# Making the second pass's V weight factors in the first pass's V stage instead of its heads

## The chip, the cores and the metric

The kernel runs on one core of a Trainium2 chip. The metric is the device time of one execution in microseconds; the median of a few runs is compared.

## The reference

One layer of a hybrid decoder block over 2048 tokens of width 1024, batch 1, all in float32. Cut to what matters here:

```python
h = rms_norm(x, g_pre) * (1.0 + scale) + shift
(pv, pg, hq, hf, hi, hg, mg_pool, mg_hgrn) = split(h @ w_in, ...)
pooled = einsum(multiscale_pool(pv), pool_w) * pool_scale
branch_a = (pooled * silu(pg)) @ w_pool_o
f = lb + (1 - lb) * sigmoid(hf);  k = 1 - f;  q = silu(hq);  v = hi
o = hgrn2(q, k, v, log(f))                    # gated linear recurrence, 8 heads of 128
branch_b = (rms_norm(o, hgrn_norm_g) * silu(hg)) @ w_hgrn_o
merged = sigmoid(mg_pool) * branch_a + sigmoid(mg_hgrn) * branch_b
x = x + gate * rms_norm(merged @ w_out, g_post)
```

The slice `hi` of `h @ w_in` (columns 3072 to 4095 of `w_in`, `O_I` in the kernel) is the V of the recurrence.

## The kernel before

The 2048 tokens are worked in two passes (`p` = 0, 1) of 1024, each pass in two halves (`t` = 0, 1) of 512. A pass goes through stages: V (the product that gives `hi`), the eight heads (for each the products for its gates, and the recurrence), A and B (the two output projections), and Y (`w_out` and the sum).

**Split products.** To keep float32 accuracy, each operand is split into a high and a low part: `split` (L175) casts to float32r on ScalarE (ACT) and subtracts on VectorE (DVE). A product of 128x128 by 128x512 then takes three matmuls on TensorE (PE), all issued at L331. Weights are loaded raw (tiles `wr`, pool of 7 buffers, L179), split into tiles `whl` (pool of 4 buffers) four items ahead of their use (`LOOK = 4`), and where the second pass needs them again, stored to DRAM.

**Fewer products.** In the heads of both passes and in V of pass 1, seven products of half-size blocks stand for eight. The blocks of `h` for this are mixed by `h_mix` (four calls, each three or four subtractions and four splits on DVE and ACT; its tiles are `t`, `hT`, `lT`). The weights of V in pass 1 need seven factors made of four blocks of `w_in`. `row_factors` makes them: for each of 4 block rows and 2 column halves ("pairs" below, eight in all) it gives seven steps:

```python
steps += [ld, nop, lambda two=two: two((0, "11"), (1, "12")),     # L295 to L299
          lambda two=two, a=sums: two(a, (2, "s1")),
          lambda two=two, a=sums2: two(a, (3, "11")),
          lambda two=two, a=sums3: two((4, "21"), a),
          lambda two=two: two((5, "12"), (6, "22"))]
```

`ld` loads two 256 KB tiles (`rav`, `rbv`, L276); the next step is empty; each `put` casts on ACT and subtracts on DVE into a tile `rfv` and stores it to DRAM (`scr_v<-rfv`, L109); `sums`, `sums2` and `sums3` are 128x256 additions and subtractions on DVE (L461).

**Where the steps are placed.** Before the change the 56 steps are the list `behind_heads`, made just before the heads of pass 0. In the heads `htick` is called about 21 times a head and takes one step at two of every five calls:

```python
def htick():                          # L1341 to L1345
    tick()
    every[0] += 1
    if every[0] % 5 in (1, 3):
        once(behind_heads)
```

What is left after the last head is taken at once (L1387). The heads of pass 1 do the same with the factors of `w_out` (`row_factors("y7", ...)`).

**The V stage of pass 0.** It is made of jobs of two 128-row weight items each (`v_job`, 24 matmuls), four jobs (`q` = 0 to 3) to a group, a group for each `t` and each half `grp` of the columns. A group accumulates in four PSUM banks (`psV`, the pool has four); its last job copies them on ACT (`V<-psV`, L888) and stores them (`Vd<-V`). The first group runs among the kernel's preparations; the other three are the loop over `vj`, twelve jobs (n = 0 to 11). Behind the jobs of the first of them three calls of `late` follow (`h_in` for the second half: scale by `rr`, shift, and split into `hB`, `lB`), behind jobs 0, 1 and 3 of the second and 0 of the third one mix each.

**What sets the order.** The code only traces the work; the framework orders each engine's instructions and inserts the waits. Nearly all working tiles (`utile`) come from one pool of 76 buffers (`NU = 76`); a tile takes a buffer at its first write. The order on SP, which issues all transfers, is also the framework's, but for those that `gated` puts behind the last store.

Of the kernel before, what the change touches and what calls it, by code (L numbers as in the profile page):

```python
# [20 lines left out]
D = 1024  # L21
# [10 lines left out]
O_PV, O_PG, O_Q, O_F, O_I, O_G, O_MP, O_MH = 0, 512, 1024, 2048, 3072, 4096, 5120, 6144  # L32
# [4 lines left out]
FAST_V, FAST_Y = True, True  # L37
# [34 lines left out]
def tile_block(ctx: ExitStack, tc: tile.TileContext, x, c, w_ada, b_ada, g_pre, g_post, w_in,  # L72
# [3 lines left out]
    V, A, G, PE, SP = nc.vector, nc.scalar, nc.gpsimd, nc.tensor, nc.sync  # L76
    x, out = x[0], out[0]
    w_ada, w_in = w_ada[0], w_in[0]
# [14 lines left out]
    def utile(name, dt=F32):  # L93
        return up.tile([P, T], dt, tag="u", name=name)

    def dram(name, shape):
        return dp.tile(shape, F32, name=name, tag=name)
# [10 lines left out]
    def store(key, dst, src):  # L108
        last["st"] = SP.dma_start(dst, src)  # L109
# [64 lines left out]
    def split(src32, hi, lo, e=None):  # L174
        return A.copy(hi, src32), (e or V).tensor_tensor(lo, src32, hi.bitcast(F32), op=SUB)  # L175
# [80 lines left out]
    def row_factors(key, src, e):  # L256

        steps = []
        W = T // 2
        for i in range(4):  # L260
            for c0 in (0, W):
                r = {}

                def put(f, nm, i=i, c0=c0, r=r):
                    w = utile(f"rf{key}{f}{i}{c0}", F32R)
                    hi, lo = w[:, 0:W], w[:, W:T]
                    split(r[nm], hi, lo, e)
                    if (key, f, i) not in scr:
                        scr[key, f, i] = dram(f"scr_{key}_{f}_{i}", [P, 2 * T])
                    store((key, f, i), scr[key, f, i].rearrange("p (z n) -> p z n", z=2)[:, :, c0:c0 + W],  # L270
                          w.bitcast(F32).rearrange("p (z n) -> p z n", z=2))

                def ld(i=i, c0=c0, r=r):
                    a, b = utile(f"ra{key}{i}{c0}"), utile(f"rb{key}{i}{c0}")
                    for w, k in ((a, 2 * i), (b, 2 * i + 1)):
                        SP.dma_start(w.rearrange("p (z n) -> p z n", z=2),  # L276
                                     src[k * P:(k + 1) * P, :].rearrange("p (z n) -> p z n", z=2)[:, :, c0:c0 + W])
                    r.update({"11": a[:, 0:W], "21": a[:, W:T], "12": b[:, 0:W], "22": b[:, W:T]})

                def sums(r=r, i=i, c0=c0):  # L280
                    r["s1"] = utile(f"rs{key}{i}{c0}")[:, 0:W]
                    tt(r["s1"], r["21"], r["22"], op=ADD, e=e)
                    tt(r["21"], r["11"], r["21"], op=SUB, e=e)

                def sums2(r=r):
                    tt(r["11"], r["s1"], r["11"], op=SUB, e=e)

                def sums3(r=r):
                    tt(r["12"], r["12"], r["11"], op=SUB, e=e)

                def two(*fs, put=put):
                    for f in fs:
                        f() if callable(f) else put(*f)
                nop = lambda: None
                steps += [ld, nop, lambda two=two: two((0, "11"), (1, "12")),  # L295
# [4 lines that stand above are left out]
        return steps  # L300
# [159 lines left out]
    def tt(o, a, b, op=MUL, e=None):  # L460
        return (e or V).tensor_tensor(o, a, b, op=op)  # L461
# [399 lines left out]
    def v_job(p, t, grp, q, cx, hook=None):  # L861
        if q == 0:
            cx["psV"] = [bank(f"psV{p}_{t}_{grp}_{tk}") for tk in range(NT)]
        pss = cx["psV"]
        it = None

        def mul(k, w, tk):
            hh, hl = cx["mv"][("B11", "B21", "B12", "B22")[2 * t + k % 2], k // 2]
            xh, xl = hh[:, tk * P:(tk + 1) * P], hl[:, tk * P:(tk + 1) * P]
            mm(pss[tk], xh, w[0], k == 0, False)  # L870
            mm(pss[tk], xh, w[1], False, False)
            return mm(pss[tk], xl, w[0], False, k == KT - 1)

        if q < 3:
            for k2 in range(2):
                w = take(2 if p == 0 and t == 0 and grp == 0 else LOOK)
                with after(it):
                    for tk in range(NT):
                        im = mul(2 * q + k2, w, tk)
                if hook is not None:  # L880
                    it = hook(2 * q + k2, im)
            return
        ws = [take(), take(LOOK - 1)]
        for tk in range(NT):
            for k2 in range(2):
                mul(2 * q + k2, ws[k2], tk)
            vt = utile(f"V{p}_{t}_{grp}_{tk}")
            A.copy(vt, pss[tk])  # L888
            store("Vd", cx["Vd"][:, t * NT + tk, grp * T:(grp + 1) * T], vt)
# [340 lines left out]
    def once(steps):  # L1230

        if steps:
            steps.pop(0)()
# [43 lines left out]
    for p in range(NPASS):  # L1277
# [39 lines left out]
        vj = [] if p > 0 and FAST_V else [(t, grp, q) for t in range(2) for grp in range(2) for q in range(4)]  # L1317
        if p == 0:
            vj = vj[4:]
        for n, (t, grp, q) in enumerate(vj):  # L1320
            if (t, grp, q) == (1, 0, 0):
                while late:
                    once(late)
            v_job(p, t, grp, q, cx)
            if t == 0:
                for _ in range(3 if p == 0 else 1):
                    once(late)
            elif q != 2:
                once(mixes)
        while mixes:  # L1330
            once(mixes)

        psa[:] = [ph.tile([P, T], F32, tag=f"ph{i}", name=f"psa{p}_{i}") for i in range(2)]
        behind_heads = []
        if p == 0 and FAST_V:
            behind_heads += row_factors("v7", w_in[:, O_I:O_I + D], V)
        if p == NPASS - 1 and FAST_Y:
            behind_heads += row_factors("y7", w_out, V)
        every = [0]
# [111 lines left out]
```

## Time and profile before

| | us |
|---|---|
| median of 3 runs | 1799.63 (1799.39 to 1804.18) |
| the profiled execution, its own time | 1797.54 |
| its span, first to last instruction | 1795.8 |
| first V products to the heads of pass 0 | 23.9 to 123 |
| heads of pass 0 | 123 to 693.8 |
| V of pass 1 | 934 to 1016.5 |
| heads of pass 1 | 1016.5 to 1569.5 |

In the profile's rows an L number is a line of the kernel, `out<-in` are the program's tile names without their numbers, and what stands in brackets is the idle time of the engine just before, with what ended it. PE is the matmul engine, PEld its weight load, SPq the queue of transfers. The granted clock of PE was 0.999.

### The profile page before, as it was taken

What the parts mean: (1) busy time and instruction counts of PE and PEld (TensorE: products, weight loads), DVE (VectorE), ACT (ScalarE), POOL (GpSimd) and SP (SyncE); (2) the same over time, 40 slices, a digit from 0 to 9 for tenths busy, and PEclk for the clock granted to TensorE, in tenths of its full rate; (3) what the DMA queues carried; (4) which work ended last, traced back from release to release, by engine and by line L of the source; (5) the groups of instructions that cost most, each with busy time, mean ns of one, the idle gap of its engine ahead of it and who ended that gap; (6) DMA issues with size and microseconds to landing.
All of it is one profiled execution on the core that took longest, in us unless ns stands there. A gap on an engine that the chain in (4) does not pass through costs nothing.

```text
span 1795.8 us, 32263 instructions
## 1 busy us (share of the span) xinstructions
PE 1753.0 (98%) x11997; PEld 1434.1 (80%) x11997; DVE 1161.1 (65%) x2522; ACT 801.1 (45%) x1925; POOL 80.6 (4%) x144
## 2 busy tenths in 40 slices
PE   7999999999999999999999999999999999999998
PEld 4787887888787787888878788888888888888886
DVE  3758898897888895475536166666666665633446
ACT  5746657566565563222433144354454453310041
POOL 1100000000000010000000000000000000000002
PEclk9999999999999999999999999999999999999999
DMA  9768787888878769997987886876877866696367
GB/s 316 255 198 292 272 295 288 277 304 281 285 271 300 265 213 318 336 323 257 320 294 249 281 254 199 282 249 215 274 228 238 280 206 238 201 351 209 129 204 258
DMA packets 270902, 471.49 MB, mean 263 GB/s; under 512 B 21101, under 2 KB 144666, under 8 KB 270746
## 3 DMA queue, kind: packets, MB, share of 16 engines
q1 hardware_dynamic: 270746, 469.44, 77.1%
q8 instruction: 94, 1.54, 0.4%
q14 instruction: 62, 0.51, 0.1%
HBM read 275.90 MB, written 193.46 MB: 261 GB/s over the span
## 4 chain that ended last, share of the span: by engine, by line
PE 62%; DMA 5%; DVE 2%; ACT 1%; issue 1%; SPq 0%; POOL 0%; DVEq 0%; ACTq 0%
PE psB L331 10%; PE pagp L331 6%; PE pam L331 6%; PE pafq L331 5%; PE psA L331 4%; PE psy L331 4%; PE pegp L331 3%; PE pefq L331 3%; PE pem L331 3%; PE psa L331 2%; PE ray L331 2%; PE po L331 2%; PE raV L331 2%; PE pbm L331 2%; PE pbfq L331 1%; PE pbgp L331 1%
## 5 line engine op out<-in xcount | busy, mean ns | idle before, releaser
L175 ACT CAST whl<-wr 128x512 fp32r<-128x512 f32 x192 | 118.5, 621 | 131.0 <-PE psB L331 24.7
L175 DVE TENSOR_TENSOR whl<-wr,whl 128x512 fp32r<-128x512 f32 x192 | 130.9, 688 | 64.2 <-ACT whl L175 55.2
L331 PE MATMUL psB<-Gh,whl 128*128 128x512 f32 x512 | 158.6, 390 | 0.0
L331 PE MATMUL pagp<-hT,whl 128*128 128x512 f32 x384 | 128.5, 395 | 4.7 <-DVE c22gp L461 3.8
L331 PE MATMUL pam<-hT,whl 128*128 128x512 f32 x384 | 129.5, 398 | 1.2 <-DVE c22m L461 1.2
L331 PE MATMUL pafq<-hT,whl 128*128 128x512 f32 x384 | 126.7, 391 | 3.3 <-ACT c12fq L592 3.3
L331 PEld LDWEIGHTS psB<-Gh,whl 128*128 128x128 f32 x512 | 96.1, 188 | 20.5 <-issue 0.5
L690 DVE COPY_PREDICATED PT<-mask,psa 128x256 f32<-128x256 uint8 x160 | 86.4, 550 | 36.1 <-PE psa L331 36.0
L331 PE MATMUL psB<-Gl,whl 128*128 128x512 f32 x256 | 100.0, 391 | 0.0
L331 PEld LDWEIGHTS pagp<-hT,whl 128*128 128x128 f32 x384 | 72.0, 188 | 21.9 <-issue 3.1
L331 PEld LDWEIGHTS pafq<-hT,whl 128*128 128x128 f32 x384 | 72.1, 188 | 19.5 <-ACT c12fq L592 4.4
L331 PEld LDWEIGHTS pam<-hT,whl 128*128 128x128 f32 x384 | 72.1, 188 | 17.2 <-DVE c22m L461 1.6
L331 PE MATMUL psA<-Ph,whl 128*128 128x512 f32 x256 | 82.5, 397 | 3.1 <-DMA Ph<-Pd 1.9
L331 PE MATMUL psV<-whl,hB 128*128 128x512 f32 x256 | 79.9, 394 | 2.4 <-ACT hB L175 2.4
L461 DVE TENSOR_TENSOR K<-K,TT 128x256 f32<-128x256 f32 x192 | 81.0, 426 | 1.8 <-PE psa L331 1.7
L331 PE MATMUL psy<-whl,mgh 128*128 128x512 f32 x256 | 80.4, 394 | 0.5 <-DVE y L461 0.5
L331 PE MATMUL pam<-lT,whl 128*128 128x512 f32 x192 | 74.9, 390 | 0.0
L331 PE MATMUL pagp<-lT,whl 128*128 128x512 f32 x192 | 74.9, 390 | 0.0
L331 PE MATMUL pafq<-lT,whl 128*128 128x512 f32 x192 | 74.7, 389 | 0.0
L331 PEld LDWEIGHTS psa<-X,K 128*32 128x32 f32 x2816 | 49.6, 110 | 25.8 <-issue 24.4
L461 DVE TENSOR_TENSOR sm<-psB,sm 128x512 f32<-128x512 f32 x32 | 22.0, 689 | 64.4 <-PE psB L331 63.9
L331 PE MATMUL psa<-X,K 128*32 128x48 f32 (+2 forms) x2816 | 60.3, 208 | 0.2 <-DVE PT L684 0.2
(471 smaller groups left out, 4417.2 us busy)
## 6 DMA issues: line engine op xcount, KB each, us to landing
wr<-in_w_in_dram SPq DMA_DIRECT2D x112, 256.0 KB, 5.0
whl<-scr_y SPq DMA_DIRECT2D x40, 512.0 KB, 4.9
sm<-Sd SPq DMA_DIRECT2D x64, 256.0 KB, 4.8
scr_v<-rfv SPq DMA_DIRECT2D x56, 256.0 KB, 2.8
whl<-scr_v SPq DMA_DIRECT2D x28, 512.0 KB, 3.7
scr_y<-rfy SPq DMA_DIRECT2D x56, 256.0 KB, 3.3
x<-in_x_dram SPq DMA_DIRECT2D x32, 256.0 KB, 4.9
wa<-in_w_ada_dram SPq DMA_DIRECT2D x32, 256.0 KB, 6.0
```

The lines of the kernel that those rows point to most:

```text
L175: return A.copy(hi, src32), (e or V).tensor_tensor(lo, src32, hi.bitcast(F32), op=SUB)
L331: return PE.matmul(o, lhsT=l, rhs=r, start=start, stop=stop, skip_group_check=True)
L461: return (e or V).tensor_tensor(o, a, b, op=op)
L690: V.copy_predicated(dst.rearrange("p (c q) a b -> p c q a b", c=NT), m, src.rearrange("p c (a b) -> p c a b", b=b).unsqueeze(2) .broadcast ...
```

## The change

The list of steps is made before the twelve V jobs of pass 0, and behind each job four steps are taken. So 48 of the 56 steps are traced in the V stage; the last eight are left for `htick` in the heads.

```diff
         if p == 0:
             vj = vj[4:]
+        behind_heads = row_factors("v7", w_in[:, O_I:O_I + D], V) if p == 0 else []
         for n, (t, grp, q) in enumerate(vj):
             if (t, grp, q) == (1, 0, 0):
                 while late:
...
                     once(late)
             elif q != 2:
                 once(mixes)
+            for _ in range(4):
+                once(behind_heads)
         while mixes:
             once(mixes)
 
         psa[:] = [ph.tile([P, T], F32, tag=f"ph{i}", name=f"psa{p}_{i}") for i in range(2)]
-        behind_heads = []
-        if p == 0 and FAST_V:
-            behind_heads += row_factors("v7", w_in[:, O_I:O_I + D], V)
         if p == NPASS - 1 and FAST_Y:
             behind_heads += row_factors("y7", w_out, V)
```

## The prediction

> **What bounds the kernel now.** I read the head of the profile first, then the stretches of the first pass, then what TensorE (PE) waited for.
>
> ```profile
> span 1795.8 us, 32263 instructions
> PE 1753.0 (98%) x11997; PEld 1434.1 (80%) x11997; DVE 1161.1 (65%) x2522; ACT 801.1 (45%) x1925; POOL 80.6 (4%) x144
> ```
>
> PE is busy for 98% of the span. A change that moves work between VectorE (DVE), ScalarE (ACT) and the transfers can gain only what PE still idles, and loses whatever makes PE wait.
>
> The stretches of pass 0: the three remaining groups of the V stage (52 to 79.5, 79.5 to 101.2, 101.2 to 123), the first 16 us of the heads, and the rest of the heads. The columns are length, then busy time of PE, PE's weight loads, DVE, ACT and POOL, the granted clock, the DMA share and the rate.
>
> ```profile
> core 0: us, PE busy (x) PEld busy (x) DVE busy (x) ACT busy (x) POOL busy (x), PEclk, DMA share, GB/s
> 52.00:79.50 27.50, 26.23 (x119) 21.03 (x118) 17.56 (x29) 23.47 (x49) 6.29 (x11) 1.00 0.70 237
> 79.50:101.20 21.70, 21.70 (x97) 18.00 (x96) 15.08 (x24) 11.39 (x21) 0.00 (x0) 1.00 0.57 178
> 101.20:123.00 21.80, 21.80 (x97) 18.03 (x97) 16.71 (x27) 11.47 (x21) 0.00 (x0) 1.00 0.48 159
> 123.00:139.00 16.00, 15.51 (x69) 12.51 (x68) 4.98 (x8) 7.93 (x13) 0.00 (x0) 1.00 1.01 350
> 139.00:693.80 554.80, 544.76 (x4446) 448.27 (x4444) 482.14 (x1096) 339.96 (x838) 30.28 (x42) 1.00 0.81 277
> ```
>
> In the last two V groups PE never rests, so any new wait there is paid in full. In the heads it idles 0.49 + 10.04 = 10.5 us, and DVE is busy for 482 of 555 us. That is the attraction of the change: the heads are crowded, the V stage is not. PE's named waits in the heads:
>
> ```profile
> PE pagp L331 <- DVE c22gp L461: 3.8, 3, 1.9
> PE pafq L331 <- ACT c12fq L592: 3.3, 4, 1.4
> PE pvm L331 <- ACT KS L777: 2.3, 2, 1.5
> PE pagp L331 <- DVE pm L461: 0.8, 1, 0.8
> ```
>
> **The change part by part.** Eight half-blocks ("pairs") of seven steps make 56 steps. Twelve V jobs now take four each, 48; eight are left for the heads. What moves is six whole pairs and the first six steps of the seventh. One pair is 2 loads, 7 casts on ACT, 7 subtractions and 4 sums on DVE, and 7 stores:
>
> ```profile
> L109 SPq DMA_DIRECT2D scr_v<-rfv x56: 518/519/2269, 144.8 to 602.5; - x56
> L175 ACT CAST rfv<-rav x24: 390/406/428, 143.6 to 588.2; 128x256 fp32r<-128x256 f32 x24
> L276 SPq DMA_DIRECT2D rav<-in_w_in_dram x8: 385/516/1332, 130.1 to 545.4; - x8
> 262.99 0.42 DVE L175 TENSOR_TENSOR rfv<-rav,rfv 128x256 fp32r<-128x256 f32 x1
> 263.32 0.42 DVE L175 TENSOR_TENSOR rfv<-rbv,rfv 128x256 fp32r<-128x256 f32 x1
> ```
>
> *Amounts.* Moved to DVE in the V stage: 6 x 11 + 9 = 75 instructions, which start 0.33 us apart when back to back, so 24.8 us. DVE already has 17.56 + 15.08 + 16.71 = 49.4 of 71 us there; together 74.2, or 3 us too much. ACT: 47 casts at 0.41 are 19 us on 46.3, fits. SP: 47 stores at 0.52 and 14 loads at about 0.5, 31 us of issuing, fits. Transfers: 61 x 0.262 MB = 16.0 MB on 27.5 x 0.237 + 21.7 x 0.178 + 21.8 x 0.159 = 13.9 MB; 29.9 MB over 71 us would be 421 GB/s, where the saturated stretch at 123 us moved 350. Taken as amounts the stage is overfull by a little. The same work leaves the heads: 25 of 487 us of DVE, and a tenth of the 159 MB.
>
> *Order.* This is the term that decides. All these tiles come from one pool of 76 buffers, and the rows suggest that its buffers are given out strictly in the order in which the code first writes them:
>
> ```profile
> 79.69 0.59 ACT L888 COPY V<-psV 128x512 f32<-128x512 f32 x1
> 80.27 0.69 DVE L461 TENSOR_TENSOR t<-h,h 128x512 f32<-128x512 f32 x1
> ...
> 87.14 0.69 DVE L461 TENSOR_TENSOR t<-h,h 128x512 f32<-128x512 f32 x1
> ...
> 96.70 0.69 DVE L175 TENSOR_TENSOR whl<-wr,whl 128x512 fp32r<-128x512 f32 x1 [2.03 <-ACT whl L175]
> 101.46 0.69 DVE L175 TENSOR_TENSOR whl<-wr,whl 128x512 fp32r<-128x512 f32 x1 [4.07 <-DMA Vd<-V]
> 102.07 0.69 DVE L461 TENSOR_TENSOR t<-h,h 128x512 f32<-128x512 f32 x1
> ...
> 108.95 0.68 DVE L461 TENSOR_TENSOR t<-h,h 128x512 f32<-128x512 f32 x1
> ...
> 101.49 0.59 ACT L888 COPY V<-psV 128x512 f32<-128x512 f32 x1
> ```
>
> The third mix (the `t` at 102.07) has had its inputs since 78 us. DVE sits idle for 4.07 us before 101.46, yet the mix starts only after the fourth V copy of the group (101.49), which the code traces just ahead of it. The first mix likewise starts at 80.27, just behind the V copy at 79.69. So I count the h_in parts, the mixes, the factor steps and the V copies as one chain. In the heads a step came every two or three ticks, so a load had many microseconds before its first cast (issued at 130.1, cast at 143.6). In the V stage four steps are traced at once: `ld` and the empty step lose their spacing, and all that is traced behind them waits until the load has landed. The V copies are among that, and they free the four PSUM banks that the next group needs at once:
>
> ```profile
> 77.48 1.54 ACT L888 COPY V<-psV 128x512 f32<-128x512 f32 x3
> 79.49 0.62 PE L331 MATMUL psV<-whl,hB 128*128 128x512 f32 x2
> ...
> 70.39 0.68 DVE L175 TENSOR_TENSOR lB<-h,hB 128x512 fp32r<-128x512 f32 x1
> DMA to landing us min/median/max: 3.0/5.1/7.0
> DMA to landing us min/median/max: 5.1/6.3/6.6
> ```
>
> The first landing row is that of the raw weight tiles (`wr`), the second that of the factor loads (line L276).
>
> *Prices of the chain.* A load that nothing covers: 5.1 (the smallest on L276) to 6.3; below, 3.0 (the smallest for `wr`), since the stage's transfers are lighter now; with its issue (0.5) I take 5.4 and 3.5. A mix with the weight splits between its parts: 108.95 - 102.07 = 6.9; without those (three of 0.6), 5.1. The work of a pair: 11 x 0.33 = 3.7, in shares by step. Four V copies: 2. What is left of an h_in when only its cast and subtraction wait: about 0.8.
>
> Group ending at 79.5. The third h_in is done at about 70 (lB at 70.39). Then load 5.4, steps of the first pair 1.5, three h_in 2.5, rest of the pair 2.2, second load 5.4 (the last two h_in lie beside it), steps 2.3: the first V copy at 89.3 instead of 77.5, and PE goes on at 89.9 instead of 79.5: 10.4 lost. With the low prices it goes on at 83.8: 4.3.
>
> Second group. Copies 2, steps 1.5, mix 6.9 (the third load is hidden beside it), steps 2.7, mix 6.9, steps 0.8, load 5.4, seven steps 3.7: 29.9 from V copy to V copy, where PE needs 21.8: 8.1 lost. Low prices: 1.8.
>
> Third group. Copies 2, mix 6.9, load 5.4, steps 1.5, mix 6.9, steps 2.2, load 5.4, steps 3.7: 34.0, so 12.2 lost. Low prices: 4.3.
>
> Sum 30.7 at the high and 10.4 at the low prices. I take 19, a little below the middle, because 20 us more of stage also spread the transfers (29.9 MB over 90 us are 332 GB/s, under the 350).
>
> *What is queued behind the waiting instructions.* ACT's next weight casts stand behind a cast that waits for its load, and DVE's behind its subtractions; with four splits ahead (11 us of PE, at 21.8/8 = 2.7 us a tile) these are covered as long as one wait stays below some 6 us. On SP the stores wait for DVE and hold the raw weight loads behind them; those run seven tiles ahead (19 us), which covers it. If either cover goes, it adds to the 19; that is why the range reaches over 30.
>
> *Heads.* One row names what is relieved there, and the chain that ended last shows such a store ahead of a weight load:
>
> ```profile
> SPq L109 <- DVE rfv L175: 64.5, 33, 6.7
> 529.33 2.40 DMA scr_v<-rfv
> 533.75 1.12 SPq L179
> 534.92 5.25 DMA wr<-in_w_in_dram
> ...
> 609.19 5.71 DMA wr<-in_w_in_dram
> 620.13 2.96 PE pagp L331 x12
> ```
>
> The factor stores held SP for 64.5 us and left with weight loads behind them; the last store is issued at 602.5, yet the wait at 620 still follows a late weight load (609.19). So part of the 10.5 us goes, not all: bounds 0 and 10.5, I take 5. The eight steps that stay cost the first head what they cost now. In the second pass the factors are read at 934 us, long after; nothing changes there.
>
> *Sum.* +19 - 5 = +14 on the profiled execution's 1797.5 us, 1811.5. Its time is 2.1 us under the median of the runs shown (1799.63), so the median becomes 1813.6.
>
> **The rivals.**
>
> *Transfers bound the stage.* If the order costs nothing by itself, 29.9 MB at the saturated 350 GB/s take 85.4 us instead of 71: +14.4, less 5 in the heads, 1809. For it: the stretch at 123 us is at share 1.01. Against it: one row of saturation, and stores that PE does not wait for can run over into the heads. [...]
>
> *Only DVE is overfull.* If the order is not strict and loads are fetched in time, the 3 us of DVE surplus runs over into the 11 idle us of DVE after 123; at most 3 us are lost, 5 gained: 1798. It covers too that the steps are made in the heads after all, because the order put them back. Against it: the idle 4.07 us before the third mix.
>
> *Faster.* The same, and all of PE's 10.5 us of idling in the heads goes, because weight loads no longer stand behind factor stores: 1789. It decides if a load in the V stage lands before its cast's turn, so that the three groups still take 27.5, 21.7 and 21.8 us. For it: 64.5 us of SP waits. Against it: the wait at 620 that has no factor store before it.
>
> **How the numbers follow.** From no change a measurement of this kernel can tell about 0.3%, 5.4 us: 1794.2 to 1805.0. Forecast (order): 0.62, 1813.6, its own range 1803 (10.4 - 7) to 1829 (30.7 - 1). Transfers: 0.14. DVE only: 0.15. Faster: 0.09. Slower: nearly all of the first two, 0.72; same: 0.18; faster: 0.10. The range 1798 to 1829 leaves out the faster rival and the tails, about 0.18.
>
> **What would show it.** Right: PE waits of 4 to 12 us at the first matmul of each of the next three groups (tiles psV, psV and pafq), released by V copies; the V stage ends at about 142 instead of 123; ACT's or DVE's waits for `rav` or `rbv` loads stand ahead of them; the rows of `rfv` lie between 70 and 160; the heads take 566 instead of 571 us. Wrong: the three groups keep their lengths (then one of the last two rivals), or the stage lengthens with PE stops spread over weight tiles (whl) and the DMA share at 1.0 (transfers).

## The result, and the profile after

The changed kernel takes 1824.9 us (median, 1821.58 to 1825.9) where the kernel before takes 1800.95 us on the same chip (1799.39 to 1804.18): a ratio of 1.0127, 95% interval 1.0107 to 1.0148. It is 24 us slower; 1813.6 was forecast, with a range up to 1829. The two profiled executions differ by 27.9 us of span (1823.7 against 1795.8). Of the six executions of heads_pool, a kernel further down, one took 4512.8 us; its ratio leaves that one out.

The head of the profile after:

```profile
span 1823.7 us, 32199 instructions
PE 1761.8 (97%) x11997; PEld 1441.1 (79%) x11997; DVE 1162.3 (64%) x2522; ACT 801.8 (44%) x1925; POOL 86.5 (5%) x144
```

DVE and ACT do as much as before (1161.1 and 801.1 us); PE is busy 8.8 us longer with the same 11997 matmuls. The other 19 us are standing still. The stretches of the V stage after, and the heads; columns as in the table of the prediction (length; busy PE, weight load, DVE, ACT, POOL; granted clock, DMA share, rate):

```profile
52.40:81.50 29.10, 27.82 (x124) 22.07 (x122) 20.80 (x40) 24.57 (x53) 6.42 (x11) 1.00 0.83 281
81.50:91.90 10.40, 0.00 (x0) 0.00 (x0) 6.09 (x15) 3.79 (x9) 0.00 (x0) 0.61 0.85 273
91.90:116.50 24.60, 24.58 (x96) 19.79 (x96) 18.49 (x35) 13.21 (x28) 0.00 (x0) 0.89 0.78 246
116.50:126.40 9.90, 0.03 (x1) 0.03 (x1) 5.71 (x16) 3.75 (x11) 0.00 (x0) 0.74 0.71 215
126.40:150.80 24.40, 24.40 (x96) 19.66 (x96) 19.36 (x36) 12.19 (x26) 0.00 (x0) 0.90 0.76 244
150.80:156.90 6.10, 0.07 (x2) 0.04 (x1) 5.85 (x14) 3.58 (x11) 0.00 (x0) 0.88 1.00 357
...
173.00:722.30 549.30, 547.86 (x4462) 452.31 (x4460) 457.36 (x1020) 327.35 (x793) 35.98 (x42) 1.00 0.74 258
722.30:1823.70 1101.40, 1084.22 (x6990) 891.59 (x6980) 602.46 (x1285) 378.14 (x933) 37.40 (x64) 1.00 0.76 255
```

Three stretches with no matmul stand behind the three groups, and the two groups that follow a stop take 24.6 and 24.4 us where 96 matmuls took 21.7. In the first two stops neither DVE (6.09 of 10.40, 5.71 of 9.90 us) nor the transfers (share 0.85 and 0.71) are full; in the third both nearly are. The timeline of PE names what ends each stop (in brackets the idle time and its releaser):

```profile
91.92 1.22 PE L331 MATMUL psV<-whl,hB 128*128 128x512 f32 x2 [10.42 <-ACT V L888]
...
126.37 1.22 PE L331 MATMUL psV<-whl,hB 128*128 128x512 f32 x2 [9.88 <-ACT V L888]
156.87 0.79 PE L331 MATMUL pafq<-hB,whl 128*128 128x512 f32 x1 [6.03 <-ACT V L888]
```

The V copies on ACT, on the first matmul of each next group, as forecast. The timeline of ACT shows what the copies stood behind:

```profile
83.77 0.40 ACT L175 CAST rfv<-rav 128x256 fp32r<-128x256 f32 x1 [0.58 <-DMA rav<-in_w_in_dram]
89.07 0.40 ACT L175 CAST rfv<-rbv 128x256 fp32r<-128x256 f32 x1 [4.89 <-DMA rbv<-in_w_in_dram]
...
91.28 2.04 ACT L888 COPY V<-psV 128x512 f32<-128x512 f32 x4
...
122.61 0.41 ACT L175 CAST rfv<-rbv 128x256 fp32r<-128x256 f32 x1 [4.83 <-DMA rbv<-in_w_in_dram]
...
125.75 2.04 ACT L888 COPY V<-psV 128x512 f32<-128x512 f32 x4
```

In both cases the wait is for the *second* load of a pair, `rbv`. The queue of SP shows why that one is so late:

```profile
80.75 0.39 SPq L276 DMA_DIRECT2D rav<-in_w_in_dram  x1
81.23 2.88 SPq L109 DMA_DIRECT2D scr_v<-rfv  x4
84.20 0.71 SPq L276 DMA_DIRECT2D rbv<-in_w_in_dram  x1
```

Four factor stores of the pair before stand between the two loads. `rbv` is issued 3.45 us after `rav`, and its first cast starts 8.3 us after `rav` was issued; the prediction's price of an uncovered load was 5.4. In the second case the two loads are issued 4.87 us apart (113.00 and 117.87), again with factor stores between them, and the cast of `rbv` starts 9.6 us after the issue of `rav`.

The bill of the span: the heads start 33.9 us later (156.87 against 123.01). Of these, 26.3 are the three stops (10.42 + 9.88 + 6.03), 5.6 the two slower groups (24.6 and 24.4 against 21.7), and 1.9 lie ahead of the change (the first group's last V copy at 57.17 against 55.30; in the kernels below this place scatters from 55.6 to 59.0 without relation to the edit). The heads then take 565.4 us (156.9 to 722.3) instead of 570.8, and the rest 1101.4 instead of 1102.0: 33.9 - 5.4 - 0.6 = 27.9.

### The profile page after: what moved, and what is told of

Read it like the earlier page. It is cut to its first block, busy times and chain, and to the rows that moved or that the text cites. A ratio compares the mean times of both kernels' runs of the same rounds, so it can differ in the third digit from the quotient of the medians.

```text
span 1823.7 us, 32199 instructions
## 1 busy us (share of the span) xinstructions
PE 1761.8 (97%) x11997; PEld 1441.1 (79%) x11997; DVE 1162.3 (64%) x2522; ACT 801.8 (44%) x1925; POOL 86.5 (5%) x144
## 4 chain that ended last, share of the span: by engine, by line
PE 85%; DMA 9%; DVE 3%; ACT 1%; SPq 1%; issue 1%; POOL 0%; DVEq 0%; ACTq 0%; POOLq 0%
PE pagp L331 10%; PE psB L331 9%; PE pam L331 9%; PE pafq L331 9%; PE pegp L331 5%; PE pefq L331 5%; PE pem L331 4%; PE psA L331 4%; PE psa L331 4%; PE po L331 3%; PE pbgp L331 2%; PE pbm L331 2%; PE psV L331 2%; PE pbfq L331 2%; PE ray L331 2%; PE raV L331 2%
## 5 line engine op out<-in xcount | busy, mean ns | idle before, releaser
L331 PE MATMUL psV<-whl,hB 128*128 128x512 f32 x256 | 84.6, 414 | 23.2 <-ACT V L888 20.3
L331 PEld LDWEIGHTS psV<-whl,hB 128*128 128x128 f32 x256 | 50.2, 199 | 37.7 <-ACT V L888 21.1
```

The costliest lines, as they stand in the source:

```text
L331: return PE.matmul(o, lhsT=l, rhs=r, start=start, stop=stop, skip_group_check=True)
```

## The experiments

Beside the experiments the kernel before takes 1797.2 to 1799.5 us, where it took 1800.95 beside the changed kernel; so what a run gained or lost is best read against the kernel before that stood beside it, and the changed kernel loses 24 us by that measure. Times are medians; those of one run have no interval.

### The order of the buffers: own_buffers

In the V stage the tiles `rfv` and the sums `rsv` come from another pool, of five buffers, so that the factor steps take fewer turns in the pool of 76 (the loaded tiles `rav` and `rbv` stay in it).

```diff
+    def ftile(name, dt=F32):
+        return qp.tile([P, T], dt, tag="qr", name=name) if apart[0] else utile(name, dt)
...
-                    w = utile(f"rf{key}{f}{i}{c0}", F32R)
+                    w = ftile(f"rf{key}{f}{i}{c0}", F32R)
...
-                    r["s1"] = utile(f"rs{key}{i}{c0}")[:, 0:W]
+                    r["s1"] = ftile(f"rs{key}{i}{c0}")[:, 0:W]
...
+            apart[0] = True
             for _ in range(4):
                 once(behind_heads)
+            apart[0] = False
```

> The changed kernel, but the factor tiles (rf) and the sums (rs) that are made in the V stage take their buffers from the pool of the recurrence (tag qr, 5 buffers, not used in the V stage) instead of the pool of 76. Same steps in the same jobs, same instructions, same transfers. Theory (the chain of the 76 buffers in program order): V copies no longer stand behind factor steps, the three stops of PE (10.4, 9.9 and 6.0 us in the changed kernel) fall to under 2 us together, the heads start at 123 to 129 us instead of 156.9 and last 565 us as in the changed kernel; time 1801 - 5 + (0 to 6) = 1796 to 1802. Rival (amounts: 74 us of DVE work and 30 MB in 71 us): the stage still takes 85 us or more, heads from 137 us on, time 1809 or more. Rival (the factor casts hold ACT's own queue, whatever the buffers): the stops stay within 3 us of what they were, time 1820 or more.

1820.14 us, ratio to before 1.0115 (1.0096 to 1.0134): nearly all of the loss is still there (22.4 of 24 us), and the expectation that the order alone is the price fell. What it gave for the rival of the amounts was met: the heads start at 145.6 (137 or later) and the time is over 1809. Of the third case only the time was met (1820 or more). But the stops changed their releaser. The waits of PE in the V stage (us in total, times, the longest):

```profile
PE psV L336 <- DVE whl L175: 8.7, 4, 5.9
PE pafq L336 <- DVE c22fq L466: 5.4, 1, 5.4
PE pafq L336 <- ACT V L893: 3.1, 1, 3.1
PE psV L336 <- ACT V L893: 2.9, 2, 1.7
```

V copies now cost 6.0 us instead of 26.3; weight tiles and a sum of the first head (`c22fq`) are late in their place. How strict the order was in the changed kernel is seen by counting the factor casts on ACT ahead of each group's V copies (rows of `rfv` alone; columns length, DVE, ACT with counts, clock, share, rate):

```profile
57.00:91.28 34.28, 3.94 (x10) 4.02 (x11) 0.89 0.80 267
91.28:125.75 34.47, 6.27 (x17) 6.12 (x18) 0.85 0.76 238
125.75:156.24 30.49, 5.36 (x15) 5.07 (x15) 0.89 0.80 265
```

The code traces 12, 28 and 44 steps ahead of the three groups' copies, which hold 11, 28 and 42 casts, so 11, 17 and 14 a group; the rows have these but for one that straddles an edge. ACT made every traced cast first. With buffers of their own the same copies came behind only 8 to 9, 21 and 38 to 42. So the shared pool does set the exact order. What that order costs by itself is not shown: the interval of this run's ratio overlaps that of the changed kernel (1.0107 to 1.0148), most of the same casts still stand ahead of the copies, and a second limit lies close under it.

### The uncovered load: loads_ahead and loads_pool

In the first, each pair's loads are traced in the empty step of the pair before. In the second, they stay in their place but are issued by POOL.

```diff
+                lds.append(ld)
...
+        if key == "v7":
+            for n in range(len(lds)):
+                if n > 0:
+                    steps[7 * n] = lambda: None
+                if n + 1 < len(lds):
+                    steps[7 * n + 1] = lds[n + 1]
```

> The changed kernel with the load of each pair traced in the empty step of the pair before, so that it has seven steps to land; all else as in the changed kernel. Theory (chain, loads uncovered): what goes is what ACT and DVE waited for rav and rbv in the V stage, 0.6 + 4.9 + 0.2 + 4.8 + 1.4 = 11.9 us on ACT, the first load stays uncovered; the sum of the stops falls from 26.3 to about 14, time about 1813 (1808 to 1818). The mixes and the steps themselves stay in the chain, so it does not return to 1801. Rival (amounts): nothing changes, 1822 to 1828. Rival (loads are the whole cause): stops under 5 us, time under 1805.

```diff
-                        SP.dma_start(w.rearrange("p (z n) -> p z n", z=2),
+                        (G if key == "v7" else SP).dma_start(w.rearrange("p (z n) -> p z n", z=2),
```

> The factors' loads (rav, rbv) are issued by POOL instead of SP, nothing else changes. In the changed kernel the second load of a pair stood on SP behind factor stores that wait for DVE, and an uncovered load took 8 to 9 us instead of 5.4. If that hold is what made it long, each of the three stops shrinks by 2 to 4 us, and the time is 1812 to 1819 us; the waits for rbv of 4.9 and 4.8 us on ACT fall to about 1. If the amount of transfers sets the landing, the waits stay and the time is 1822 to 1827.

1816.16 us (one run) and 1815.25 us (ratio 1.0095, 1.0074 to 1.0117). Against the kernel before beside them 18.4 and 16.7 of the 24 us are left, and the waits of 4.9 and 4.8 us for `rbv` are gone from ACT. What is left of the stops with the loads ahead:

```profile
86.05 1.22 PE L339 MATMUL psV<-whl,hB 128*128 128x512 f32 x2 [6.11 <-ACT V L896]
117.03 1.22 PE L339 MATMUL psV<-whl,hB 128*128 128x512 f32 x2 [6.66 <-ACT V L896]
```

The third stop is 2.25 us there, but the first head then waits 5.1 us for a weight tile. With the loads on POOL the stops are 6.3, 4.3 and 4.3. So a quarter to a third of the loss was loads that nothing covered. The queue of POOL holds a surprise:

```profile
72.92 0.72 POOL L276 DMA_DIRECT2D rav<-in_w_in_dram  x1
75.05 0.73 POOL L276 DMA_DIRECT2D rbv<-in_w_in_dram  x1 [1.40 <-DVE h L461]
76.73 0.72 POOL L276 DMA_DIRECT2D rav<-in_w_in_dram  x1 [0.96 <-DVE rfv L175]
```

The load at 76.73 is that of the third pair. The code traces it behind the first group's V copies, which came at 87.91: on a queue with little else in it, a load ran past them. The order of the buffers is therefore not a lock on everything; it acts through each engine's own order (ACT's casts above), and on SP a load also stood behind the stores ahead of it (`rbv` at 84.20, behind four stores that took 2.88 us). This run takes away both the hold and the late place, so it doesn't tell the two apart.

### The stores on another queue: stores_pool

```diff
-                    store((key, f, i), scr[key, f, i].rearrange(...)
+                    (G.dma_start if key == "v7" else SP_store)(scr[key, f, i].rearrange(...)
```

> The factors' stores are issued by POOL instead of SP; the loads stay on SP, which is then never held by a store that waits for DVE. If SP's hold makes the loads long, this gives what moving the loads gives (1812 to 1819 us), and the heads lose none. If the weight loads (wr) are held as well, it gives more: 1805 to 1812. If only the amount of transfers counts: 1822 to 1827, as the bytes are the same.

1815.47 us (1.0097, 1.0076 to 1.0117), as much as moving the loads, and no more (the stops are 7.5, 6.8 and 4.0): the further gain for the raw weight loads did not come, in line with the prediction's cover for them. The change of queue saved 7 us of 1825, and not the issue alone: in the first case above four stores took SP 2.9 us, of which 4 x 0.52 are issue, but in the second SP first waited 3.1 us (113.50 to 116.64) for DVE's result, and the load behind the stores with it.

### The amount of transfers: stored_twice

Every factor of the changed kernel is stored a second time to a place that nobody reads.

```diff
+                    if key == "v7":
+                        if ("dup", f, i) not in scr:
+                            scr["dup", f, i] = dram(f"dup_{f}_{i}", [P, 2 * T])
+                        store(("dup", f, i), scr["dup", f, i].rearrange(...)
```

> The changed kernel with every factor tile stored a second time, to a place that nobody reads: 47 more stores of 0.262 MB in the V stage, 12.3 MB. Theory (chain): a second store costs what SP's queue holds ahead of a factor load, some 0.5 us for each store that stands there, and buffers that come back later: 3 to 10 us in all, time 1828 to 1835. Rival (transfers bound the stage): 12.3 MB at 350 GB/s are 35 us more, time 1855 or more. Rival (DVE's amount bounds it): no change, 1822 to 1828.

1851.42 us (one run), 26.5 more than the changed kernel, or 29.7 when each is read against the kernel before beside it, for 12.3 MB more in the V stage: far above the 3 to 10 of the chain alone, and not quite the 35 of the saturated rate. The stops grew to 13.3, 17.2 and 13.3 us, with the same releaser, so a store's price is paid through the V copies.

### Both mends, and what is under them: own_ahead, own_dve_twice, own_stored_twice

`own_ahead` joins the edits of own_buffers and loads_ahead.

> Both mends together: the factors' tiles take buffers of their own, and the loads of a pair are traced in the empty step of the pair before. Alone the first gave 1820 and the second 1816 us where the changed kernel takes 1825. If the order of buffers and the uncovered loads are the whole price, the stage goes back to about 71 us and the heads keep their gain of 5: 1793 to 1800. If the amount of transfers is a floor below that (29.9 MB at 350 GB/s are 85 us instead of 71), 1805 to 1810. If DVE's amount (74 us of work in 71) is the floor, 1798 to 1803.

1815.26 us (1.0099, 1.0083 to 1.0114). All three cases of the expectation (up to 1810) were too low: the two mends don't add up, and 16.7 of the 24 us are left. Two rows of ACT bear on why:

```profile
ACT rfv L175 <- DMA scr_v<-rfv: 5.8, 3, 2.4
...
146.41 2.04 ACT L901 COPY V<-psV 128x512 f32<-128x512 f32 x4
```

The first is a wait that the mend itself brought: with five buffers a cast must wait until an older factor's store has landed; the changed kernel has no such wait in its V stage. The second shows that the V copies are not free: these four stand behind 44 factor casts, the last two at 142.81 and 145.59, and PE's last matmul of the group had ended at 142.46. So the words "no order of buffers is left in it", in the next expectation, say too much. The next two put a dose on top of this kernel, of DVE work alone and of stores alone.

```diff
                     split(r[nm], hi, lo, e)
+                    if apart[0]:
+                        V.tensor_tensor(lo, r[nm], hi.bitcast(F32), op=SUB)
```

> The kernel with both mends (own buffers, loads ahead; 1815.3) takes some 92 us for the stretch that took 71 before, though no order of buffers is left in it. What is the floor? Here each of the 47 factor subtractions of the V stage is made twice on DVE with the same result; no byte and no cast is added. They start 0.33 us apart back to back and take 0.42 alone: 15.5 to 20 us more of DVE. If DVE's amount bounds the stage, 1829 to 1835 us. If the transfers bound it, DVE has some 18 of 93 us to spare there, and it is 1815 to 1820. In between: DVE binds in a part of the stage.

The other has the edit of stored_twice.

> On the same kernel with both mends, every factor is stored a second time to a place that nobody reads: 12.3 MB more in the V stage, no more work for DVE and ACT; 47 more stores of 0.52 us on SP. If transfers bound the stage at the 350 GB/s of the saturated stretch, it is 35 us longer, about 1850; by what the same dose cost in the changed kernel (26.5 us), 1842. If DVE bounds it, the extra bytes fill up what the share of 0.86 leaves (some 4.5 MB in 93 us) and run over into the heads: 1815 to 1825.

The V stage behind the first group, in own_ahead, own_dve_twice and own_stored_twice (the rows end 1 to 4 us ahead of the heads, which start at 147.0, 149.2 and 169.1):

```profile
52.00:146.00 94.00, 80.11 (x322) 62.55 (x320) 74.96 (x152) 61.91 (x136) 6.43 (x11) 0.92 0.86 286
```

```profile
52.00:145.00 93.00, 77.23 (x300) 60.80 (x299) 82.53 (x182) 58.37 (x127) 6.15 (x11) 0.89 0.85 279
```

```profile
52.00:168.00 116.00, 84.72 (x320) 64.94 (x320) 79.61 (x156) 63.88 (x135) 6.30 (x11) 0.86 0.97 327
```

47 more subtractions on DVE cost 2 us (1817.34, 1.0099, 1.0078 to 1.012, against 1815.26). 12.3 MB more cost 25 us (1840.59, 1.0228, 1.0207 to 1.0249), and the share goes from 0.86 to 0.97. With the dose on DVE the stops move to weight tiles that DVE splits (10.8 us of PE's waits, from 1.6), so DVE is not far from binding either. Stores cost far more than DVE work, but this doesn't show that the amount of transfers is what holds own_ahead at 1815 us. The second store keeps each of the five buffers longer, as this row of own_stored_twice shows:

```profile
121.76 0.41 ACT L175 CAST rfv<-rbv 128x256 fp32r<-128x256 f32 x1 [2.67 <-DMA dup<-rfv]
```

From 84 to 145 us there are eleven such waits for a store to land on ACT, 13.0 us together. The second store also puts 47 issues of 0.52 us on SP, which this run doesn't part from the bytes. And without the dose the share is 0.86, not 1, so no full pipe runs through the whole stage. What holds own_ahead stays open: bytes, SP's queue, the five buffers, or the casts ahead of the copies. In stored_twice, whose buffers are the 76, the dose cost as much (26.5 us); so the five buffers are not needed for the price of a dose.

### Half the dose: two_steps

```diff
-            for _ in range(4):
+            for _ in range(2):
                 once(behind_heads)
```

> Two steps behind each of the twelve V jobs instead of four: 24 of the 56 are made in the V stage, 32 stay in the heads. By the chain of buffers the price hangs on where a load falls, not on the amount: ahead of the first group's V copies stands one load instead of two (the load that was still waited for until 89.07 goes), so those copies come at about 81 instead of 91.3 and the stop shrinks from 10.4 us to 2 to 5; the next two loads are traced just ahead of a mix that covers them, so the second and third stop go (under 2 us each). With half of the heads' gain (2.7 us) that is 1797 to 1802 us. If the amount of transfers or of DVE work sets the price, half of the steps cost about half of 27 us: 1808 to 1813, or, if the amount only binds above a threshold (22 MB over 71 us are 310 GB/s, under the 350), nothing: 1795.

1800.97 us, ratio 1.0014 (1.0003 to 1.0025): half of the steps cost a tenth of the loss. That fits the place of the loads as well as a limit that binds only above some amount, and excludes a price in proportion (1808 to 1813). The first V copies came at 80.5 (expected at about 81) and the first stop, expected at 2 to 5 us, is gone; stops of 1.8 and 1.2 us behind V copies are left. Yet the heads gained nothing: 572.7 us against 570.8, in a profiled execution that at 1804.55 us is 3.6 above the median. Waits of PE in them:

```profile
PE pafq L331 <- ACT c12fq L592: 2.8, 1, 2.8
PE pafq L331 <- DVE c22fq L461: 2.2, 1, 2.2
PE pvm L331 <- ACT KS L777: 1.9, 1, 1.9
```

### The slow matmuls behind a stop: pe_kept_busy

Matmuls of no use (44, 50 and 34) fill the three stops.

```diff
+            if (t, q) == (1, 0):
+                spin(44 if grp == 0 else 50)
             v_job(p, t, grp, q, cx)
...
+        if p == 0:
+            spin(34)
         v_head(p, 0, cx)
```

> The changed kernel with 44, 50 and 34 extra matmuls of 128x128 by 128x512 (0.227 us each, results unused) traced ahead of the second and third V group and of the heads, where PE stops. Asked is why the 16 to 20 matmuls after each stop take 0.42 us instead of 0.23. Theory (PE slows down because it stood still): with PE kept busy the granted clock stays at 1.0 and each group takes 21.8 us again instead of 24.5; the V copies come when the chain lets them, at about the same times, so little is gained: 1819 to 1825. Rival (the matmuls after a stop wait for late weights or banks): groups stay at 24 to 25 us.

1824.56 us (one run) against 1824.9: nothing. The stretches between V copies (the useless matmuls included in PE's count), and the first matmul behind the first stop:

```profile
90.50:122.40 31.90, 31.30 (x139) 25.84 (x139) 24.17 (x50) 16.79 (x38) 0.00 (x0) 1.00 0.82 257
122.40:154.30 31.90, 31.65 (x140) 25.88 (x138) 25.41 (x52) 15.63 (x35) 0.00 (x0) 1.00 0.76 257
...
91.15 0.74 PE L331 MATMUL psV<-whl,hB 128*128 128x512 f32 x2 [0.60 <-ACT V L888]
```

The granted clock stays at 1.00 and the matmuls at full speed (0.23 us from start to start), but the V copies come 31.9 us apart, whatever PE does: the sum for the last two groups is 63.8 us against 34.5 + 30.5 = 65.0 in the changed kernel. So the 5.6 us of slower matmuls in the bill are not a loss of their own; they take the place of idle time that the late copies would have made.

### Where the heads' gain comes from: heads_pool

The kernel *before*, all steps in the heads, with the edit of stores_pool alone.

> The kernel before with one edit: the factors' stores are issued by POOL instead of SP; all steps stay in the heads. It asks where the heads' gain of 5.4 us came from. If the stores' hold on SP (64.5 us of waits with weight loads behind) is what the factors cost in the heads, nearly the same gain comes without moving anything: 1792 to 1796 us. If it is the amount of DVE work in the heads (25 us of 487), nothing changes: 1797 to 1800.

1793.62 us, ratio 0.996 (0.9945 to 0.9975): faster than both kernels. The heads before, and in this kernel, and what PE still waits for in the latter's heads:

```profile
123.00:693.80 570.80, 560.27 (x4513) 460.78 (x4511) 487.12 (x1103) 347.89 (x851) 30.28 (x42) 1.00 0.81 279
```

```profile
126.30:690.90 564.60, 559.22 (x4513) 461.27 (x4511) 485.81 (x1103) 347.82 (x851) 72.93 (x98) 1.00 0.82 282
...
PE pvm L334 <- ACT KS L780: 1.9, 3, 0.7
PE pagp L334 <- DVE pm L464: 1.3, 1, 1.3
PE psa L334 <- DVE K L464: 1.0, 1, 1.0
PE pafq L334 <- ACT c12fq L595: 0.7, 1, 0.7
```

564.6 us, a little less than the 565.4 of the change, with DVE as busy in the heads as before (485.81 us). So the heads' loss came with the stores on SP's queue, not with the amount of DVE work. It isn't the length of SP's waits either: in the heads those for `whl` grew from 115.8 to 171.5 us, while those for `rfv` fell from 64.5 to 33.5. By which transfer the stores held PE up was not traced.

### Both together: two_ahead_pool

Two steps behind each job, loads ahead, stores on POOL.

> Two steps behind each V job, the loads traced a pair ahead, the factors' stores issued by POOL. With everything left in the heads, the stores on POOL alone gave 1793.6 us, and two steps alone 1801.0. If the heads' loss came from the stores on SP and not from DVE's work, there is nothing left to gain by moving steps: at best the same 1792 to 1796, and up to 1799 where some 8 MB more in the V stage delay a copy or a weight tile. If the amount of work in the heads costs something besides, moving 24 steps gives a further 1 to 3 us: 1789 to 1792.

1804.64 us, ratio 1.0039 (1.0026 to 1.0053): slower than before, and outside every case of the expectation. In the profiled execution (1808.43 us, 3.8 above the median) the stops in the V stage are short (1.9 and 2.0 us), but the first head has one of 4.5, for the sum `c22fq`. The timeline of ACT and of DVE there, and ACT's row at the same place in the kernel before:

```profile
152.46 0.62 ACT L178 CAST whl<-wr 128x512 fp32r<-128x512 f32 x1 [6.84 <-DMA scr_('fq', 0)_2_1492<-whl]
```

```profile
153.11 0.69 DVE L178 TENSOR_TENSOR whl<-wr,whl 128x512 fp32r<-128x512 f32 x1 [10.26 <-ACT whl L178]
...
154.05 0.68 DVE L472 TENSOR_TENSOR c22fq<-pafq,c22fq 128x512 f32<-128x512 f32 x1
```

```profile
133.75 0.62 ACT L175 CAST whl<-wr 128x512 fp32r<-128x512 f32 x1 [3.94 <-DMA scr_('fq', 0)_2_1351<-whl]
```

The first head stores its split weights to DRAM, and a `whl` buffer (there are four) is free only once its store has landed. That already holds ACT for 3.94 us before the change, at a share of 1.01. Here it is 6.84 us; DVE stands behind ACT for 10.26 us with the sum close behind, and PE waits for the sum. The store itself is issued late, at 145.42, behind two loads (`pvt`) that took SP 4.6 us to issue where they took 2.1 before. own_buffers shows the same chain (7.22 us on ACT, then the 5.4 us for `c22fq` in its waits). So what is put at the end of the V stage meets the full pipe of the first head (share 0.99 from 139 to 154 us).

## Why the prediction was right, and where its sizes were off

*Sign and mechanism* were right. The three stops lie where it said, on psV, psV and pafq, released by V copies; ACT waits for `rbv` ahead of two of them, and 42 of the 56 casts into `rfv` lie between 75 and 156 us, as forecast, the rest up to 222. The order of tracing is the order on ACT, cast for cast. One sentence of it was too strong: that all that is traced behind a load waits for it. The third pair's load, on a queue of its own, passed the V copies by 11 us. Nor is the order shown to be the whole price: with both mends 16.7 of the 24 us are left. So it is partly luck that the time fell where the order's sum put it.

*The stops.* 10.4, 8.1 and 12.2 at the high prices, 4.3, 1.8 and 4.3 at the low; measured 10.4, 9.9 and 6.0, sum 26.3. The step that was mis-sized is "I take 19": the sum lay near the high end. One part is arithmetic: with the low prices as listed (a load 3.5, a mix 5.1) the three groups come to 6.6, 2.6 and 4.8, 14.0 in all and not 10.4, which would have put the middle at 22. The reason for going below the middle was that a longer stage spreads the transfers, and it left out what SP does between the two loads of one pair. It priced a pair's load as one landing of 5.4 us; with factor stores between `rav` and `rbv` it was 8.3 and 9.6 us from the first issue to the second cast. The text had seen that stores hold the raw weight loads behind them, and had not asked the same of the factor loads. The third stop came out at half of its price; from V copy to V copy the last group took 30.5 us instead of 34.0. The trace shows two parts of that: its first mix starts at 126.30, beside the V copies and not behind them, and the casts of its first load (135.08 and 135.49) waited for no load, since both halves had been issued at 130.6 and 131.3, beside that mix.

*The V stage's end.* Forecast at 142, measured at 156.9: 7 us are in the stops, 5.6 in the slower matmuls behind them, 1.9 ahead of the change.

*Amounts.* The prediction counted 47 factor stores and 14 loads into the stage, 16.0 MB. The four steps traced behind the last job stand behind the last V copies, so 42 factors and 12 loads were made ahead of them, and the rates above give 13.4 MB more than before. Nor is 350 GB/s a ceiling here: the kernel before moved 364 GB/s at a share of 1.07 from 23.9 to 52 us.

*Covers that held.* The raw weight loads and the four splits ahead: behind the first tile of the heads only one wait of 1.0 us for a `whl` tile remains, and taking the stores off SP gave no more than taking the loads off.

*The heads.* Forecast -5 and 566 us, measured -5.4 and 565.4. The 5 was a choice between bounds of 0 and 10.5, so that it came this close is luck. The reason given, the stores on SP, got its test in heads_pool: moving them alone gave 6.2 us there.

*The rivals.* Transfers (1809): not the bound of the changed kernel's first two stops, which have shares of 0.85 and 0.71, but not excluded as the next limit under it: with order and loads mended it is still 1815, more stores cost 25 us, and the first head's full pipe turns late stores into waits. The rival's price of 14 assumed the saturated rate over the whole stage, while own_ahead moved 286 GB/s there. DVE alone (1798): excluded by the time; and 47 more subtractions cost only 2 us. Faster (1789): the heads' gain was half of PE's idling there, and the V groups did not keep their lengths; the way to that gain left the V stage alone.

## What to carry to other kernels

Before moving work into a stage that looks half empty, write out each in-order queue behind it: in the changed kernel the copies that free the accumulators stood behind all of the 11, 28 and 42 casts traced ahead of them, and `rbv` was issued 3.45 and 4.87 us after `rav`, behind factor stores, the latter time behind 3.1 us in which SP waited for DVE's result. Here spare engine time (DVE was busy for 6.09 of the 10.40 us of the first stop) was not spare queue time, and the transfers added at the end of the V stage in two_ahead_pool met those at the start of the heads (share 0.99, a stop of 4.5 us). Where stores that wait share a queue with loads that others wait for, try the stores on the queue of an engine that is idle first (POOL was busy for 4%): that one edit gave 0.4% here, while moving the work cost 1.3%.

## What the hardware showed that was not expected

After each of the three stops of the changed kernel (10.42, 9.88 and 6.03 us) the matmuls ran at nearly half speed for about 5 us. The timeline of PE behind the first stop, two weight tiles apart:

```profile
95.50 0.63 PE L331 MATMUL psV<-whl,lB 128*128 128x512 f32 x1
95.92 1.05 PE L331 MATMUL psV<-whl,hB 128*128 128x512 f32 x2
...
97.74 0.39 PE L331 MATMUL psV<-whl,lB 128*128 128x512 f32 x1
97.97 0.61 PE L331 MATMUL psV<-whl,hB 128*128 128x512 f32 x2
```

One matmul takes 0.42 us from start to start (95.50 to 95.92), and 0.23 from 97.74 on. The slow part is 91.92 to about 97.2, 126.37 to 131.2 and 156.87 to 162.2: 5.3, 4.9 and 5.3 us, and some 2.4 to 2.6 us longer each time than the same matmuls at 0.23; the granted clock of the two groups is 0.89 and 0.90. Stops of 1.8 us (two_steps) and 2.25 us (loads_ahead) were followed by full speed (0.23 us from start to start) within a microsecond; one of 3.07 us (own_ahead) by slow matmuls for almost 6 us. But the length of the stop alone doesn't decide. In two_ahead_pool a stop of 1.85 us is followed by slow matmuls, 0.43 us from start to start, for 3.5 us:

```profile
84.82 1.13 PE L342 MATMUL psV<-whl,hB 128*128 128x512 f32 x2 [1.85 <-ACT V L899]
```

And in own_ahead a stop of 3.24 us is followed by full speed for 1.2 us (85.90 to 87.10), and a further stop of 1.15 us by slow matmuls for 5.7 us (88.25 to 93.94). In pe_kept_busy, where the stops are filled, none of the three places has slow matmuls: behind each they start 0.23 us apart. What sets the length of the slow part is not shown.
